# A two-layer decoder trunk on one core: the chunk inverse of the delta rule built ahead as one packed matrix

## The chip, the cores and the metric

The kernel runs on one core of one Trainium2 chip. Everything is float32 at the boundary. The metric is the device time of one execution in microseconds; the time shown of the kernel before is the median of three runs. A core has TensorE (PE, matmuls into PSUM), VectorE (DVE), ScalarE (ACT), GpSimd (POOL) and SyncE (SP); the last two serve here mainly as queues that issue DMAs. Each engine works through its own instructions in the order in which the program lists them.

## The reference

Input is x of 256 tokens by 2048 features. Layer 0 mixes tokens by gated DeltaNet (16 query/key heads, 32 value heads, head size 128), layer 1 by sparse attention; each layer then has a gated MLP with a short convolution (width 5120), two layer norms and a gated embedding. The change lies in layer 0's mixer. Its core is, per value head and chunk of C tokens:

```python
lmat = jnp.where(strict, jnp.einsum('bhncd,bhnsd->bhncs', kb, k) * decay, 0.0)
amat = lmat + jnp.eye(C, dtype=jnp.float32)
rhs = jnp.concatenate([vb, kb * jnp.exp(gc)[..., None]], axis=-1)
sol = lax.linalg.triangular_solve(amat, rhs, left_side=True, lower=True, unit_diagonal=True)
```

`k` is the key after a causal convolution of four taps, silu and division by its norm; `kb` is `beta * k`. What follows from `sol` is a recurrence over the chunks: the values that remain after the state's own prediction (`u` below), the output of each chunk, and the state's update. Every head's output is then normalized, gated by silu(z) and multiplied by `w_o`.

## The kernel before

**Products.** All large matmuls are made exact enough by splitting each float32 operand into a rounded part `hi` and a rest `lo`, both in a rounded format. A weight block (512 KB) is loaded by SP into one of three `raw` buffers, ScalarE makes `hi` (L406), VectorE makes `lo` (L414), and PE multiplies: `wide` columns at L343 and L346 (weights stationary, 256 tokens of both parts streaming), narrow ones at L356 to L359. Small products of the mixer are plain float32 matmuls.

**The order of the work.** Nothing is scheduled by hand. The class `Plan` is a list scheduler that runs when the kernel is built: each piece of work is added with `add(engine, cost, emit, after, take, give, rank, tail)`. `cost` is its assumed time on the engine, `tail` the assumed time until a DMA has landed, `take` and `give` name buffers, and among the pieces that can start the smallest `rank` goes first. The ranks stand in the table `RANK` (L165). The result is a fixed list of instructions for each engine. The large products form one chain in program order (`place`, `multiply`); small PE pieces with rank 1 are put between the weight blocks wherever the plan has them ready.

**The mixer's stages.** The 32 value heads form eight groups of four heads (two key heads each), groups 0 to 3 in batch 0 and 4 to 7 in batch 1. The kernel's chunk is 128 tokens, so there are two halves (`a`), and an inverse of 128 x 128 per head and half.

- `batch(b)` (L826) makes the strict lower matrices `L` for four groups: decays come by DMA from a row table and pass through ScalarE (`decays`, `fade`), the key's squared norms are summed by `squares` (ScalarE squares, PE multiplies by ones, L786), `newton` takes the inverse root, the gram matrix of the keys is a PE product (L863), and for batch 1 ScalarE multiplies `L` by the scales (`dim`) and VectorE by the gram (`weigh`, L880). The 32 x 32 diagonal blocks of `L` are stored to HBM (L890), loaded with one block per partition (L896), inverted there by 31 steps of VectorE (L914, L916) and stored as `tt` (L919).
- `front(g)` (L922) makes what needs the queries: norms, the products of keys and queries, masked and decayed.
- `group(g)` (L961) solves for `u`. It fills the block-diagonal matrix `pm` with the inverses of the 32-row blocks by four DMAs (L991), multiplies `L` by it and masks the result to get `W` (`inverse`, `mask`, L1003), and then solves by rounds: `begin` multiplies the right-hand side by `pm`, ScalarE moves the result to `y0` (L1035), and three times PE multiplies by `W` (`apply`, through `mul` at L959) and VectorE subtracts (`less`, L1050). Since `W` has four blocks by four, three rounds are exact. This is done for half 0; then `cross` takes its part out of half 1's right-hand side and the same is done for half 1.
- After `u`, the output product (L1066, L1067), norms, gating (L1097), transposes on PE (L1106), and the split result in `oT`, which `mixes` multiplies by `w_o`.

The groups are spread over the projections: the loop at L1142 runs, for each group, the columns of values, keys, queries and gates that come next, and `mixes` of the group before, while `group(g)` and `front(g + 1)` are put in between by the plan. PSUM has four banks for the large products, two tagged `sp` and two tagged `bk` for the small ones. `L` has five buffers; one of them is taken as `lt` in batch 0.

**Later stages.** Layer norms are written in `norm` (L1265): VectorE (or ScalarE, by the ranks `even`, `put`, `round`, `held`) evens x, PE transposes it, and the result is split again.

Of the kernel before, what the change touches and what calls it, by code (L numbers as in the profile page):

```python
# [8 lines left out]
F32 = mybir.dt.float32  # L9
# [7 lines left out]
P = 128  # L17
# [146 lines left out]
class Trunk:  # L164
# [16 lines left out]
            'round': 1,  # L181
# [46 lines left out]
    def build(self, out):  # L228
# [5 lines left out]
                                qd=2, qo=2, n21=2, sq=1, L=5, pm=1, W=1, u=1, y0=1, y=2, wq=2,  # L234
# [17 lines left out]
        pm, W = new("pm", [8, P]), new("W", [2, 4, P])  # L252
# [6 lines left out]
        nc.gpsimd.memset(W, 0.0)  # L259
# [565 lines left out]

        def batch(b):  # L826
# [11 lines left out]
            d = [squares(K[g], finished("k", K[g]), lambda ps, i=i: nc.vector.tensor_scalar(  # L838
                ss()[:, 4 * i:4 * i + 4], ps, RMS_EPS, None, op0=ALU.add)) for i, g in enumerate(gs)]
            d, rk = newton(ss, 16, d)  # L840

            def scales():
# [9 lines left out]
                s["tt"] = self.dr.tile([4, 8, 4, 32, 32], F32, tag="tt", name="tt")  # L852
            d = s["d"] = add(V, 1.0, scales, [d, rows["go"]], rank=2)
            stored = []
            for i, g in enumerate(gs):
                box = {}

                def gram(g=g, box=box):
                    ps = box["ps"] = sps("sp", [2, 2, P], "l_ps")
                    for a in range(2):  # L860
                        kt = K[g]()[:, :, a * P:(a + 1) * P]
                        for j in range(2):
                            nc.tensor.matmul(ps[:, a, j], kt[:, j], kt[:, j], start=True, stop=True)  # L863
                p = add(E, 0.9, gram, finished("k", K[g]) + [d], take=["sp"], rank=1)
                grams[g] = p
                for a in range(2):
# [11 lines left out]
                    def weigh(a=a, g=g, box=box):  # L878
                        l = five(L[g]()[:, a])
                        nc.vector.tensor_tensor(l, bcast(box["ps"][:, a], 2, 2), l, op=ALU.mult)  # L880
# [934 lines left out]
```

## Time and profile before

| | before |
|---|---|
| median of three runs | 2794.57 us (2793.72 to 2796.26) |
| the profiled execution | 2794.5 us, span 2792.7 |
| PE busy | 2781.3 us, 15100 matmul records |
| VectorE, ScalarE, POOL busy | 1887.7, 1425.5, 104.9 us |
| granted PE clock | 1.000 |
| moved by DMA | 519.63 MB, mean 186 GB/s |

The span runs from the first to the last instruction of the profiled execution; its time has the start and end of the launch around that. "Busy" is the union of an engine's instructions. Matmuls overlap one another in the records (each lasts until its result is out), so the distance from one start to the next is what PE is occupied for, not the duration shown. Each plain float32 matmul leaves two records. In a row of the timeline the first number is the start in microseconds from the beginning of the span, the second the duration; `x8` means eight records merged.

### The profile page before, as it was taken

The page shows a single profiled execution, that of the slowest core. Times are in us where ns is not written, and L with a number is a line of the kernel's source. Part 1 is how long each engine was busy: PE and PEld are TensorE (multiplying, and loading weights), DVE is VectorE, ACT ScalarE, POOL GpSimd, SP SyncE. Part 2 cuts the span into 40 slices and gives each one's busy share as a digit, 9 for nine tenths or more (in the row PEclk, how much of TensorE's full clock was granted, in tenths as well). Part 3 has the DMA queues.
Part 4 walks back from the last instruction along what each step waited for, and adds up shares of the span by engine and source line. Part 5 has one row for each costly group of instructions (what it writes and reads, how often), then busy time and mean ns, then how long its engine had stood idle before and what let it go on. Part 6 is the DMA issues. An engine that isn't in the chain of part 4 may idle for free.

```text
span 2792.7 us, 39922 instructions
## 1 busy us (share of the span) xinstructions
PE 2781.3 (100%) x15100; PEld 2404.7 (86%) x15100; DVE 1887.7 (68%) x2947; ACT 1425.5 (51%) x2263; POOL 104.9 (4%) x177
## 2 busy tenths in 40 slices
PE   9999999999999999999999999999999999999999
PEld 8888888888888888888888888988888888888887
DVE  7877778776777666666545766776766666654575
ACT  5755665555544555555433444455455555543343
POOL 0100001000000000000000000210000000000000
PEclk9999999999999999999999999999999999999999
DMA  7765656655545766666556557554656666655655
GB/s 223 212 176 166 181 150 185 171 157 167 154 133 167 217 206 209 206 198 189 194 194 221 174 168 226 170 163 158 217 157 193 200 195 192 195 193 191 210 174 189
DMA packets 408929, 519.63 MB, mean 186 GB/s; under 512 B 20348, under 2 KB 298208, under 8 KB 408736
## 3 DMA queue, kind: packets, MB, share of 16 engines
q1 hardware_dynamic: 401424, 499.81, 58.5%
q0 software_dynamic: 6624, 16.68, 2.1%
q8 instruction: 118, 1.93, 0.3%
q14 instruction: 75, 0.61, 0.1%
q10 hardware_dynamic: 688, 0.59, 0.1%
HBM read 512.76 MB, written 7.39 MB: 186 GB/s over the span
## 4 chain that ended last, share of the span: by engine, by line
PE 96%; DVE 2%; DMA 1%; ACT 0%; issue 0%; ACTq 0%; DVEq 0%
PE mm_ps L346 33%; PE mm_ps L343 17%; PE b_ps L359 13%; PE b_ps L356 13%; PE b_ps L357 13%; PE s_ps L959 2%; DMA raw<-in_gdn_w_in 1%; PE o_ps L1067 1%; PE w_ps L959 0%; DVE lo L414 0%; PE ss_ps L786 0%; PE lg_ps L1638 0%; PE sc_ps L1555 0%; PE o_ps L1066 0%; PE l_ps L863 0%; PE v_ps L976 0%
## 5 line engine op out<-in xcount | busy, mean ns | idle before, releaser
L414 DVE TENSOR_TENSOR lo<-raw,hi 128x1024 fp32r<-128x1024 f32 (+1 forms) x906 | 1103.4, 1220 | 683.6 <-ACT hi L406 676.8
L406 ACT ACTIVATE hi<-raw 128x1024 fp32r<-128x1024 f32 (+1 forms) x876 | 922.8, 1054 | 1122.2 <-PE mm_ps L346 519.5
L346 PE MATMUL mm_ps<-xT,hi 128*128 128x512 f32 (+1 forms) x4136 | 1014.0, 393 | 1.6 <-DVE pd L556 1.1
L346 PEld LDWEIGHTS mm_ps<-xT,hi 128*128 128x128 f32 (+1 forms) x4136 | 755.1, 188 | 148.8 <-ACT v L567 1.5
L343 PEld LDWEIGHTS mm_ps<-xT,lo 128*128 128x128 f32 (+1 forms) x4136 | 531.1, 191 | 20.7 <-ACT xb L1310 0.3
L343 PE MATMUL mm_ps<-xT,lo 128*128 128x256 f32 (+1 forms) x4136 | 544.2, 283 | 0.1
L356 PE MATMUL b_ps<-hi,xT 128*128 128x512 f32 (+2 forms) x678 | 260.2, 385 | 0.4 <-ACT hi L406 0.4
L357 PE MATMUL b_ps<-hi,xT 128*128 128x512 f32 (+2 forms) x678 | 257.5, 381 | 0.0
L356 PE MATMUL b_ps<-hi,hTA 128*128 128x512 f32 x512 | 199.2, 389 | 0.0
L357 PE MATMUL b_ps<-hi,hTA 128*128 128x512 f32 x512 | 199.2, 389 | 0.0
L359 PE MATMUL b_ps<-lo,xT 128*128 128x512 f32 (+2 forms) x678 | 180.1, 382 | 0.0
L356 PEld LDWEIGHTS b_ps<-hi,xT 128*128 128x128 f32 x678 | 127.4, 188 | 24.3 <-ACT hi L406 0.8
L357 PEld LDWEIGHTS b_ps<-hi,xT 128*128 128x128 f32 x678 | 127.4, 188 | 23.0
L359 PEld LDWEIGHTS b_ps<-lo,xT 128*128 128x128 f32 x678 | 124.7, 188 | 23.0
L359 PE MATMUL b_ps<-lo,hTA 128*128 128x512 f32 x512 | 136.9, 389 | 0.0
L356 PEld LDWEIGHTS b_ps<-hi,hTA 128*128 128x128 f32 x512 | 96.1, 188 | 20.0
L357 PEld LDWEIGHTS b_ps<-hi,hTA 128*128 128x128 f32 x512 | 96.1, 188 | 20.0
L359 PEld LDWEIGHTS b_ps<-lo,hTA 128*128 128x128 f32 x512 | 96.1, 188 | 19.9
L356 PE MATMUL b_ps<-hi,oT 128*128 128x512 f32 (+1 forms) x258 | 103.5, 401 | 0.0
L357 PE MATMUL b_ps<-hi,oT 128*128 128x512 f32 (+1 forms) x258 | 100.6, 390 | 0.0
L563 DVE SCALAR_TENSOR_TENSOR ac<-pd,cw,ac 128x256 f32<-128x256 f32 x192 | 91.0, 482 | 3.8 <-ACT ac L560 0.2
L1393 DVE SCALAR_TENSOR_TENSOR fac<-fpd,fcw,fac 128x256 f32<-128x256 f32 x160 | 74.2, 482 | 2.6
(320 smaller groups left out, 2458.1 us busy)
## 6 DMA issues: line engine op xcount, KB each, us to landing
raw<-in_gdn_w_in SPq DMA_DIRECT2D x191, 512.0 KB, 4.0
raw<-in_ffn_w_down SPq DMA_DIRECT2D x160, 512.0 KB, 4.1
raw<-in_ffn_w_up SPq DMA_DIRECT2D x158, 512.0 KB, 3.9
raw<-in_ffn_w_gate SPq DMA_DIRECT2D x157, 512.0 KB, 4.4
raw<-in_dsa_w_in SPq DMA_DIRECT2D x72, 512.0 KB, 3.7
raw<-in_gdn_w_o SPq DMA_DIRECT2D x64, 512.0 KB, 3.7
raw<-in_ple_w_gate SPq DMA_DIRECT2D x56, 512.0 KB, 4.4
raw<-in_dsa_w_o SPq DMA_DIRECT2D x32, 512.0 KB, 4.5
```

Source lines behind the costliest of these rows:

```text
L343: nc.tensor.matmul(ps[o][:m, S:], lo[:, k, o * P:o * P + m], xk[:, 0], start=False, stop=e)
L346: nc.tensor.matmul(ps[o][:m], hi[:, k, o * P:o * P + m], xk.rearrange("p a b -> p (a b)"), start=s, stop=e)
L356: nc.tensor.matmul(ps[o][:, c], xh, hi[:, k, c], start=s, stop=False)
L357: nc.tensor.matmul(ps[o][:, c], xl, hi[:, k, c], start=False, stop=False)
L359: nc.tensor.matmul(ps[o][:, c], xh, lo[:, k, c], start=False, stop=e and c.stop == n)
L406: nc.scalar.activation(hi, box["raw"], AF.Copy)
L414: nc.vector.tensor_tensor(lo, box["raw"], box["hi"].bitcast(F32), op=ALU.subtract)
L563: nc.vector.scalar_tensor_tensor(box["ac"], pd[:, k:k + S], wt[:, k:k + 1], box["ac"], op0=ALU.mult, op1=ALU.add)
L959: nc.tensor.matmul(ps[:, h], lhs[:, h], rhs[:, h], start=True, stop=True)
L1067: nc.tensor.matmul(ps[:, h], qd()[:, a, h], u()[:, a, h], start=not a, stop=True)
L1393: x = add(V, 0.48, lambda k=k, pd=pd, ac=ac, m=m: nc.vector.scalar_tensor_tensor(ac(), pd()[:, k:k + S], w["taps"](k, m), ac(), op0=ALU.mu ...
```

## The change

The solve by rounds is replaced by a multiplication with the full inverse, and the full inverse is made ahead, in `batch`, by a new function `solve(s, i)` for each of the four groups. With 32-row blocks, let D be the inverses of the diagonal blocks (known as before) and G the inverse. G's blocks are found from the last block row upwards: for d = 2, 1, 0, the row d of G is minus D of d times the sum over e > d of L[e, d] times row e of G (all transposed, as the kernel holds them). The four heads of a group (and half) are packed: their 32 x 32 blocks stand on the diagonal of one 128 x 128 operand, so that one matmul serves four heads, with 32 to 96 columns streaming.

- `Lb` holds the off-diagonal blocks of `L`, six pairs (e, d) per half. They are stored to HBM by three DMAs per group (`keep`, table `lo`) and fetched by eight (`left`). `L` is free after that; it has four buffers instead of five.
- `Gc` holds G. Its diagonal blocks are fetched from `tt` by eight DMAs, its other blocks come from PE through ScalarE copies.
- `Tb` holds the transposed inverses. They are made by one transposing ScalarE copy per batch, stored as `tu`, and fetched by eight DMAs per group.
- For each d, PE multiplies by `Lb` (`left`), ScalarE copies (`keep`), PE multiplies by `Tb` (`right`), ScalarE negates and copies (`less`). Then one DMA stores Gc.
- `group(g)` fills `pm` with the upper triangle of the inverse by eight DMAs, `begin` multiplies once, and ScalarE copies the result to `u`. `W`, `y0`, `y`, `inverse`, `mask`, `apply` and VectorE's `less` are gone.
- For batch 1 the gram product is issued before the norms, and the squared norms are read from its diagonal by VectorE (`diagonals`), which replaces `squares` for those keys; `weigh` comes before `dim`.
- `front`'s gram product also waits for its decays.
- Fourteen ranks and due times change, and three are new.

The core of the diff:

```diff
-            'due': 3,
-            'tap': 3.6,
-            'rows': 3.5,
+            'due': 2,
+            'tap': 4.5,
+            'rows': 1.5,
-            'solve1': 3.7,
+            'solve1': 5,
-            'weigh1': 3,
-            'dim': 4,
+            'weigh1': 5,
+            'dim': 2,
-            'wild': 5,
+            'wild': 4,
-            'put': 0,
-            'round': 1,
+            'put': 1,
+            'round': 0.6,
-            'held': 0,
-            'even': 8,
-            'last': 0,
+            'held': 1,
+            'even': 16,
+            'last': 1,
-            'free': 2,
-            'after': 4,
-            'cast0': 9}
+            'free': 3,
+            'after': 2,
+            'cast0': 9,
+            'fill': 0.5,
+            'keep': 2,
+            'fetch': 3}
...
+            def diagonal():
+                tmp = new("xt", [256])
+                for n in range(4):
+                    a, j = n // 2, n % 2
+                    nc.vector.scalar_tensor_tensor(tmp[:, :P], box["ps"][:, a, j], 1.0, self.ident, op0=ALU.mult,
+                                                   op1=ALU.mult, accum_out=ss()[:, 4 * i + 2 * j + a:][:, 0:1])
...
+        def solve(s, i):
...
+                def left(q=q, a=a, hs=hs):
+                    nc.gpsimd.dma_start(out=Lb[hs, a, :, hs], in_=s["lo"][i, q])
+                back.append(add(G, 0.55, left, s[i] if not q else [], behind=back[-1:], take=["Lb"] * (not q), tail=3.0, rank=R["keep"]))
...
+            for what in range(2):
+                for q in range(8):
+                    back.append(add(G, 0.55, lambda q=q, what=what: fetch(q, what), [s["u"] if what else s["t"]],
+                                    behind=back[-1:], take=["Tb" if what else "Gc"] * (not q), tail=3.0, rank=R["fetch"]))
+            y = back
+            for d in (2, 1, 0):
+                n = 32 * (3 - d)
...
+                    for a in range(2):
+                        for e in range(d + 1, 4):
+                            nc.tensor.matmul(ps[:, a, 32 * (e - d - 1):], Lb[:, a, PAIR[e, d]], Gc[:, a, e, 32 * e:],
+                                             start=e == d + 1, stop=e == 3)
...
+                    nc.scalar.activation(Gc[:, :, 3, :n], box["ps"], AF.Copy)
...
+                    for a in range(2):
+                        nc.tensor.matmul(ps[:, a], Tb[:, a, d], Gc[:, a, 3, :n], start=True, stop=True)
...
+                    nc.scalar.activation(Gc[:, :, d, 32 * (d + 1):], box["ps"], AF.Identity, scale=-1.0)
+                y = add(E, 0.41 * (3 - d) + 0.05, left, y if d == 2 else [y], take=["bk"], give=["Lb"] * (not d), rank=1)
+                y = add(A, 0.2 + 0.0018 * n, keep, [y], give=["bk"], rank=1)
+                y = add(E, 0.46, right, [y], take=["bk"], give=["Tb"] * (not d), rank=1)
+                y = add(A, 0.2 + 0.0018 * n, less, [y], give=["bk"], rank=1)
...
+            s["st", i] = add(G, 0.6, store, [y], give=["Gc"], tail=3.5)
...
-                L[g] = lazy(lambda: new("L", [2, 4, P], 5))
+                L[g] = lazy(lambda: new("L", [2, 4, P], 4))
...
-            p = add(E, 1.75, gram, qe + finished("k", k) + [d, grams[g]], take=["sp", "sp"], give=["q", "k"], rank=1)
+            p = add(E, 1.75, gram, qe + finished("k", k) + [d, grams[g], *dec], take=["sp", "sp"], give=["q", "k"], rank=1)
...
+            for d in range(4):
+                for a in range(2):
+                    def fill(a=a, d=d):
+                        nc.gpsimd.dma_start(out=pm[32 * d:32 * d + 32, 4 * a:4 * a + 4, 32 * d:],
+                                            in_=s["g", i][:, :, a, d, 32 * d:].rearrange("h j c -> j h c"))
+                    ld.append(add(G, 0.55, fill, [s["st", i]], behind=ld[-1:], take=["pm"] * (not ld), tail=3.0, rank=R["fill"]))
...
-                for n in range(3):
...
-                    def apply(a=a, y=y, box=box):
-                        box["ps"] = sps("bk", [4, P], "s_ps")
-                        mul(W[:, a], y(), box["ps"])
...
-                    def less(nxt=nxt, y0=y0, box=box):
-                        nc.vector.tensor_tensor(nxt(), y0(), box["ps"], op=ALU.subtract)
...
+                d = add(A, 0.6, keep, [x], take=["u"] * (not a), give=["bk"], rank=1)
```

More of the change, by code (lines that the diff above doesn't have):

```diff
@@ L251, in build @@
         w = new("xi", [1024])
-        pm, W = new("pm", [8, P]), new("W", [2, 4, P])
+        pm, Tb, Lb, Gc = new("pm", [8, P]), new("Tb", [2, 3, P]), new("Lb", [2, 6, P]), new("Gc", [2, 4, P])
+        PAIR = {(e, d): e * (e - 1) // 2 + d for e in range(1, 4) for d in range(e)}
         pads = [new(f"pd{i}", [3 + S]) for i in range(2)]
@@ L824, in fade, with gram, product @@
             return r
+        def gram(g, box, deps=()):
+            def product():
+                ps = box["ps"] = sps("sp", [2, 2, P], "l_ps")
+                for a in range(2):
+                    kt = K[g]()[:, :, a * P:(a + 1) * P]
+                    for j in range(2):
+                        nc.tensor.matmul(ps[:, a, j], kt[:, j], kt[:, j], start=True, stop=True)
+            grams[g] = add(E, 0.45, product, finished("k", K[g]) + [*deps], take=["sp"], rank=1)
+            return grams[g]
@@ new lines, in diagonals, with weigh @@
+        def diagonals(g, i, dec, ss):
+            box = {}
+            p = gram(g, box)
+            def diagonal():
[4 more added lines that the diff above has]
+                                                   op1=ALU.mult, accum_out=ss()[:, 4 * i + 2 * j + a:][:, 0:1])
+            d = add(V, 0.9, diagonal, [p], rank=2)
+            for a in range(2):
+                def weigh(a=a):
+                    l = five(L[g]()[:, a])
+                    nc.vector.tensor_tensor(l, bcast(box["ps"][:, a], 2, 2), l, op=ALU.mult)
+                p = dec[a] = add(V, 0.69, weigh, [d, dec[a]], give=["sp"] * a, rank=R["weigh1"])
+            return d
@@ L837, in batch @@
             ss = lazy(lambda: small("kss", 16))
-            d = [squares(K[g], finished("k", K[g]), lambda ps, i=i: nc.vector.tensor_scalar(
-                ss()[:, 4 * i:4 * i + 4], ps, RMS_EPS, None, op0=ALU.add)) for i, g in enumerate(gs)]
+            if b:
+                d = [diagonals(g, i, dec[g], ss) for i, g in enumerate(gs)]
+            else:
+                d = [squares(K[g], finished("k", K[g]), lambda ps, i=i: nc.vector.tensor_scalar(
+                    ss()[:, 4 * i:4 * i + 4], ps, RMS_EPS, None, op0=ALU.add)) for i, g in enumerate(gs)]
             d, rk = newton(ss, 16, d)
@@ L855, in batch @@
             for i, g in enumerate(gs):
[L856 to L865, printed above, removed]
+                box, p = {}, None
+                if not b:
+                    p = gram(g, box, [d])
                 for a in range(2):
@@ L893, in batch, with keep @@
                     stored.append(add(G, 0.6, store, [p], tail=2.5))
+                s[i] = [p]
+                for e in range(1, 4):
+                    def keep(e=e, g=g, i=i):
+                        nc.gpsimd.dma_start(
+                            out=s["lo"][i, :, :, PAIR[e, 0]:PAIR[e, 0] + e].rearrange("q i d j -> i q (d j)"),
+                            in_=L[g]()[32 * e:32 * e + 32, :, :, :32 * e].rearrange("p a h j -> p (a h) j"))
+                    s[i].append(add(G, 0.6, keep, [p], give=["L"] * (e == 3), tail=3.0, rank=R["keep"]))
             ld = lazy(lambda: new("ld", [32, 32]))
@@ L903, in batch @@
             z = add(G, 1.2, clear, [d])
-            lt = lazy(lambda: new("L", [32, 32], 5))
+            lt = lazy(lambda: new("L", [32, 32], 4))
             if not b:
@@ L920, in batch @@
                          [d], tail=4.0)
+            d = add(A, 1.1, lambda: nc.scalar.activation(ld().rearrange("p c j -> p j c"), xi(), AF.Copy), [d], rank=1)
+            s["u"] = add(G, 0.6, lambda: nc.gpsimd.dma_start(out=s["tu"].rearrange("g q b c j -> (g q b) c j"), in_=ld()),
+                         [d], tail=4.0)
+            for i in range(4):
+                solve(s, i)
         def front(g, after=()):
@@ L965, in group @@
             last = g == 7
-            vt = lazy(lambda: new("L" if last else "vt", [2, 4, P], 5 if last else 1))
+            vt = lazy(lambda: new("L" if last else "vt", [2, 4, P], 4 if last else 1))
             key = "k" if last else "v"
```

70 lines of the change are left out of this document (34 added, 36 removed).

## The prediction

> **What bounds the kernel now.** I read the page's totals first, then the chain, then what TensorE (PE) waited for, then the sequence of its instructions.
>
> ```profile
> span 2792.7 us, 39922 instructions
> PE 2781.3 (100%) x15100; PEld 2404.7 (86%) x15100; DVE 1887.7 (68%) x2947; ACT 1425.5 (51%) x2263; POOL 104.9 (4%) x177
> ...
> PE 96%; DVE 2%; DMA 1%; ACT 0%; issue 0%; ACTq 0%; DVEq 0%
> ```
>
> A busy PE is not yet a PE at its peak, so the waits decide. Here are the longest ones of PE and of its weight loads:
>
> ```profile
> PE w_ps L266 <- DVE pd L256: 1.2, 1, 1.2
> PE mm_ps L346 <- DVE pd L556: 1.1, 1, 1.1
> ...
> PEld n_ps L1299 <- DVE x L1287: 2.9, 13, 0.5
> PEld mm_ps L346 <- DVE xT L1328: 1.5, 2, 0.8
> ```
>
> (Each row: who waited for whom, microseconds in all, times, longest.) No wait totals 3 us in 2793. PE is fed from end to end, so the time moves by the PE work that is taken out or put in, plus any wait that is new. VectorE at 68% and ScalarE at 51% of the span bound nothing by themselves.
>
> **The price of the PE work.** The pieces concerned, grouped by operation, and four places in PE's sequence that show what they cost:
>
> ```profile
> L959 PE MATMUL s_ps<-y,W 128*128 128x128 f32 x384 | 50.7, 275 | 0.0
> L786 PE MATMUL ss_ps<-cst,sq 128*128 128x1 f32 x128 | 15.1, 239 | 0.0
> L959 PE MATMUL w_ps<-pm,L 128*128 128x96 f32 x128 | 16.2, 272 | 0.0
> ```
>
> ```profile
> 214.63 1.02 PE L959 MATMUL w_ps<-pm,L 128*128 128x96 f32 x8
> 215.43 1.17 PE L346 MATMUL mm_ps<-xT,hi 128*128 128x512 f32 x4
> 216.44 2.06 PE L343 MATMUL mm_ps<-xT,lo 128*128 128x256 f32 x16
> 218.34 2.00 PE L346 MATMUL mm_ps<-xT,hi 128*128 128x512 f32 x8
> ...
> 227.95 1.98 PE L346 MATMUL mm_ps<-xT,hi 128*128 128x512 f32 x8
> 229.77 0.60 PE L976 MATMUL v_ps<-ident,v 128*128 128x128 f32 x4
> ...
> 574.29 1.05 PE L959 MATMUL s_ps<-y,W 128*128 128x128 f32 x8
> 575.10 1.17 PE L346 MATMUL mm_ps<-xT,hi 128*128 128x512 f32 x4
> 576.11 0.39 PE L356 MATMUL b_ps<-hi,oT 128*128 128x512 f32 x1
> ...
> 609.96 0.95 PE L786 MATMUL ss_ps<-cst,sq 128*128 128x1 f32 x8
> 610.76 2.16 PE L343 MATMUL mm_ps<-xT,lo 128*128 128x256 f32 x16
> 612.76 0.63 PE L346 MATMUL mm_ps<-xT,hi 128*128 128x512 f32 x2
> ```
>
> The durations overlap (matmuls are pipelined), so I price from start to start. Each f32 matmul of the program leaves two records: 8 groups x 2 halves x 3 rounds x 4 heads = 192 products of W, and 384 records. A 512-column record in a run costs (229.77 - 227.95)/8 = 0.2275 us; a 256-column one (218.34 - 216.44)/16 = 0.119. A block of 8 records then costs what it adds until the fourth record after it: 576.11 - 574.29 - 4 x 0.2275 = 0.91 us with 128 columns, 216.44 - 214.63 - 0.91 = 0.90 with 96, and 612.76 - 609.96 - 16 x 0.119 = 0.90 with one column. The width does not matter below 128: 0.113 us a record.
>
> **Removed on PE.** The three rounds of W per half: 384/8 x 0.91 = 43.7 us. The products that make W: 128/8 x 0.90 = 14.4. The sums of squares of keys 4 to 7: four blocks, 3.6. Together 61.7 us. The gram matrices of the keys are only moved ahead of the norms; `begin` keeps its size.
>
> **Added on PE.** `solve` has, per group, 2 x (1 + 2 + 3) products with Lb and 2 x 3 with Tb: 18 matmuls, 36 records; 288 records for 8 groups. Their widths of 32 to 96 columns are not in the trace, but they lie between the 1-column and the 96-column rows, which agree: 288 x 0.113 = 32.5 us. They come as six blocks per group, of 4, 4, 8, 4, 12 and 4 records; should each of the 48 blocks carry 0.1 us of its own, 5 us more. Below, I allow 0.100 us a record, 29 us.
>
> Net on PE: 61.7 - 32.5 = **29.2 us less** (24 to 33).
>
> A rule stands against the flat price: the Trainium skill, "TensorE: Matmul & The Clock Gate", section "Back-to-back issue gap", gives columns/2.4 + 2.5 ns with a floor near 25 ns, an estimated 9 us for all 288 records and some 53 us of gain. The one-column row answers it: 0.90 us for 8 records. Its section on LDWEIGHTS, 128 columns/1.2 = 107 ns whatever streams past, is what the trace agrees with.
>
> **Other engines, all beside PE.**
>
> ```profile
> 0.00:836.00 836.00, 831.63 (x4788) 726.08 (x4789) 627.03 (x1125) 479.67 (x926) 47.15 (x86) 1.00 0.60 173
> ...
> L1050 DVE TENSOR_TENSOR y<-y,s_ps 128x512 f32<-128x512 f32 x32 | 21.9, 685 | 25.0 <-PE s_ps L959 24.9
> ...
> L1035 ACT ACTIVATE y<-s_ps 128x512 f32<-128x512 f32 x16 | 9.5, 596 | 19.2 <-PE s_ps L959 19.2
> ...
> L906 ACT ACTIVATE L<-ld x1: 2073/2073/2073, 119.6 to 119.6; 128x1024 f32<-128x1024 f32 x1
> ```
>
> The first row is the linear-attention stage (engines in the page's order, then clock, DMA share, GB/s). VectorE loses 48 subtractions of 0.685 us (33 us) of 627; the sixteen products that pick the diagonals, even at the price of such a subtraction, bring 11 back. ScalarE gains at most 48 copies of 0.596 us, the price of 512 columns (28.6 us), and two transposing copies of 2.07, on 480 of 836. Both are covered. Bytes added per group: 192 KB kept, 192 for Lb, 224 for Gc and Tb, 512 stored, 320 filled, less 128 filled before; with the second inverse store some 11.5 MB in all, 14 GB/s on 173. Covered by the three raw buffers; uncovered, each weight load that came late would show as a PE wait, of which there is none now.
>
> **The new wait.** A chunk inverse now goes through POOL's queue three times: its 32-row blocks are fetched into Gc and Tb, the packed result is stored, and `pm` is filled from the store. Queued behind a late piece on PE are the weight blocks of the next groups; behind a late piece on POOL, the fetches of the next solve, and for these PE's `begin`.
>
> The DMA view (size, median us to landing), and the landings of the DMAs of `pm`:
>
> ```profile
> pm<-tt POOLq DMA_DIRECT2D x32, 32.0 KB, 3.1
> tt<-xi POOLq DMA_DIRECT2D x2, 512.0 KB, 4.7
> ...
> DMA to landing us min/median/max: 2.0/3.1/6.7
> ```
>
> The timeline of POOL, PE and VectorE around groups 0 and 4 (start, duration):
>
> ```profile
> 159.54 0.56 POOL L919 DMA_DIRECT2D tt<-xi  x1 [44.62 <-DVE ac L563]
> 165.10 2.35 POOL L991 DMA_DIRECT2D pm<-tt  x4 [5.00 <-DMA tt<-xi]
> ...
> 533.52 0.56 POOL L919 DMA_DIRECT2D tt<-xi  x1 [91.46 <-DVE xi L916]
> ...
> 177.15 1.08 PE L959 MATMUL s_ps<-vt,pm 128*128 128x128 f32 x8
> ...
> 202.98 0.69 DVE L1050 TENSOR_TENSOR u<-y,s_ps 128x512 f32<-128x512 f32 x1 [0.57 <-PE s_ps L959]
> ...
> 213.87 1.12 DVE L1097 SCALAR_TENSOR_TENSOR zs<-o_ps,rs,zs 128x128 f32<-128x128 f32 x4
> 225.81 1.38 PE L1106 MATMUL ot_ps<-ident,zs 128*128 128x128 f32 x8 [0.94 <-DVE n L946]
> 240.77 0.48 PE L356 MATMUL b_ps<-hi,oT 128*128 128x512 f32 x1
> ...
> 571.52 1.05 PE L959 MATMUL s_ps<-vt,pm 128*128 128x128 f32 x8
> 577.03 1.05 PE L959 MATMUL s_ps<-y,W 128*128 128x128 f32 x8
> ```
>
> For group 0: the inverse is stored from 159.5 and landed at 165.1. POOL issues in 2.35/4 = 0.59 us each: 16 fetches for Gc and Tb end at 174.5, landed at 177.6 with the median of 3.1. The copy for Tb (2.07 + 0.6 + 4.7 from 159.5: 166.9) is in time. The six products of `solve` alternate with ScalarE copies; one such hop, from a product over its eviction to the next product with weight blocks between, takes 577.03 - 574.29 = 2.74 us: 194.0. Store, 0.6 + 4.7: 199.3. Eight fills, 4.7 + 3.1: 207.1, where `begin` stood at 177.15 before. From there to u took 203.7 - 177.15 = 26.5; six hops fall away (16.4), leaving 10.1: u at 217.2 instead of 203.7, and the output, 213.87 + 1.12 - 203.7 = 11.3 later, at 228.5 instead of 215.0. But the transposes of it ran only at 225.81 then, held for a PSUM bank that `front(1)` had taken (the wait on n L946), and `front` now asks for it after its decays. So they come 2.7 us later, and the first matmul that reads oT, at 240.77, needs them and 4 us of copies: 233. Some 7 us are spare, and PE takes weight blocks meanwhile. Group 4: 533.5 + 47.6 = 581.1 against 571.5, with 16.4 less behind it: not late. The solves of a batch follow one another in 9.4 + 3.1 + 16.4 + 5.3 = 34 us, since Gc is one buffer: group 1's `pm` is full by 199.3 + 34 + 7.8 = 241, about where the 240.77 row stands, again with 16.4 less behind it; later groups gain some 30 us each.
>
> With the slowest landings (6.7 for 3.1 twice, for 4.7 once) the chain grows by 9 us, and 2 us of stall remain per batch; with hops a microsecond longer too, 8. I take 2 us in all, of 0 to 16.
>
> **Ranks and moved steps.** The landings of the weight loads (`raw`) in the first 836 us:
>
> ```profile
> DMA to landing us min/median/max: 3.6/4.0/11.6
> ```
>
> The ranks only order what an engine does next; those of VectorE and ScalarE (`tap`, `due`, `dim`, `weigh1`, `solve1`, `calm`, `wild`, `last`) move work on engines with a quarter or more of their time free. `rows` puts 16 loads of 512 KB two weight blocks earlier on SP's queue, ahead of raw loads; L comes free earlier, after its kept rows land, so SP waits there less. Raw loads in this stage took up to 11.6 us to land with no PE wait on them, so I price it 0, up to 5. The gram of keys 4 to 7 now takes a PSUM bank before its decays are sure to be there and holds it until `weigh`: 0, at worst what `front` cost by the same hold, 1 us each for four. For the norms (`even`, `put`, `round`, `held`), the quoted n_ps and xT waits, 4.4 us, are all that can be won; moving two more pieces to ScalarE at four places could lose as much. 0, within 5.
> **Sum.** The profiled execution took 2794.5 us, 1.8 around its span, and the median is 2794.57. 2794.5 - 29.2 + 2 = **2767**.
>
> **Rivals.** *Narrow matmuls cost by their width.* By rows, 256 columns less save 0.2275 - 0.119 = 0.108 us, so 32, 64 and 96 columns would cost 0.024, 0.038 and 0.051; with 128, 96 and 64 records of them 10 us: 2794.5 - 61.7 + 10 + 2 = 2745. The one-column row speaks against it. 5%. (By the gap rule of the page above, this is what would happen.)
>
> *Half the gain is lost at the batch starts*: the first group of each batch comes 8 us late, and oT, zs and the PSUM pair of the gates with it, so that PE has no free bank to go on in: 2794.5 - 29.2 + 16 = 2781. For it: the old chain was already awaited at 225.81; against: 7 us spare. 13%.
>
> *PE meets the DMAs sixteen times, late*: every group has a first product after the fetches and a `begin` after the fills, placed in PE's written order for a landing of 3.0 us, with all later weight blocks queued behind and VectorE and ScalarE behind those. At the longest landing each is 3.7 us late. From 29.2/16 = 1.8 us each the gain is gone, from 2.2 the kernel is measurably slower; at 2.5 the time is 2794.5 - 29.2 + 40 = 2805. For it: 256 more issues on POOL, in order. Against: eight such meetings exist now, and PE waits for none. 9%. The Trainium skill, "SBUF — State Buffer", section "SBUF: two separate sides", speaks for it: VectorE's two-port copies lock POOL out of writing descriptors; the quoted issues, 0.59 us in every batch of four, show none of it.
>
> *The ranks undo it*, with PE's work gone but the norms slower: within 0.2% of before, 2%.
>
> **Chances.** The forecast has 71%, its own range 2760 to 2776. The range 2752 to 2786 adds the case of the batch starts and the upper price of the records; left out are the cheap records, the slower rival and the tails of the rest, 2 in 10 at most. About 0.2% (5.6 us) is what a measurement of this kernel can tell from no change. Faster: 0.71 + 0.05 + 0.11 = 0.87; same 0.05; slower 0.08.
>
> **What would show it.** PE should have 15100 - 384 - 128 - 32 + 288 = 14844 matmul records; the products with Lb and Tb should cost 0.113 us a record from start to start; PE's waits should stay under some 10 us; the 836 us of the first stage should shrink by about 27 and the rest stay. Wrong would be PE waiting for ScalarE's Gc or for pm (the two late rivals), or n_ps waits grown.

## The result and the profile after

The changed kernel takes 2775.69 us (median of 4 runs, 2770.41 to 2777.85) against 2795.41 for the kernel before beside it: a ratio of 0.9923, with a 95% interval of 0.9911 to 0.9935. It is 19.7 us faster, where 27.5 were forecast. A second series, again beside the kernel before, gave 0.9924 (0.9911 to 0.9936). The profiled execution took 2776.15 us, with a span 18.4 us shorter than before.

The page's totals and chain, as shown of before:

```profile
span 2774.3 us, 39795 instructions
PE 2754.7 (99%) x14844; PEld 2378.9 (86%) x14844; DVE 1855.8 (67%) x2908; ACT 1439.3 (52%) x2314; POOL 250.4 (9%) x437
...
PE 95%; DMA 3%; POOL 1%; DVE 1%; issue 0%; SPq 0%; ACT 0%; ACTq 0%; DVEq 0%
```

The count of matmul records is the forecast 14844. PE is still the bound, but DMAs now take 3% of the chain that ends last, for 1% before, and POOL is new in it. What PE waited for (us in total, times, longest):

```profile
PE b_ps L362 <- ACT hi L412: 3.7, 2, 2.5
PE s_ps L1057 <- DMA pm<-gs: 2.8, 2, 2.2
PE mm_ps L352 <- DVE pd L562: 1.7, 1, 1.7
PE s_ps L894 <- DMA Tb<-tu: 1.4, 1, 1.4
...
PE s_ps L1057 <- DMA Gc<-tt: 0.5, 1, 0.5
```

Weight blocks that come late cost 3.7 us (first row), for 0.4 before. The waits for the operand `pm` and for the fetched blocks Tb and Gc are new, 4.7 us together. (For whom a wait was is inferred from the order of events; the row that names Tb is read again below.)

The price of the new products, from PE's timeline (start, duration):

```profile
637.84 0.53 PE L894 MATMUL s_ps<-Gc,Lb 128*128 128x32 f32 x4
638.21 1.18 PE L365 MATMUL b_ps<-lo,xT 128*128 128x512 f32 x4
...
647.52 1.42 PE L894 MATMUL s_ps<-Gc,Lb 128*128 128x96 f32 x12
648.78 0.48 PE L362 MATMUL b_ps<-hi,xT 128*128 128x512 f32 x1
...
650.69 0.58 PE L903 MATMUL s_ps<-Gc,Tb 128*128 128x96 f32 x4
651.05 0.48 PE L362 MATMUL b_ps<-hi,xT 128*128 128x512 f32 x1
```

From start to start, blocks of 4 and of 12 records take 0.37 and 1.26 us: (1.26 - 0.37)/8 = 0.111 us for each further record. Four records with 32 columns cost 0.37, with 96 columns 0.36: the width does not matter. So the 288 records cost 288 x 0.111 = 32 us and PE's work fell by 61.7 - 32 = 29.7 us. The span fell by 18.4. **Eleven microseconds of new waiting were to be found.**

A view by stretches shows the part that the list of waits does not show. The columns are: stretch, its length, the busy time of PE, its weight loads, VectorE, ScalarE and POOL, then the granted clock, the DMA share and GB/s. Around the wait for `pm` of group 4:

```profile
577.57:580.98 3.41, 3.41 (x17) 2.83 (x16) 2.41 (x4) 3.11 (x6) 2.35 (x5) 1.00 1.03 189
580.98:584.40 3.42, 1.18 (x7) 0.70 (x6) 2.07 (x4) 0.24 (x1) 1.81 (x4) 1.00 1.11 221
584.40:587.81 3.41, 3.41 (x13) 3.02 (x13) 0.43 (x1) 1.71 (x3) 3.36 (x7) 0.50 0.61 173
```

PE is idle for 2.2 us, and then works for 3.41 us at half the clock. That happens three times in this execution, from 185.04, 584.40 and 850.64 us on, and costs about half of 3 x 3.41, 5.1 us, where PE would have been busy. The profiled execution of the kernel before had it only in its last moments.

Where the rest of the gain lies shows at a landmark behind the first stage, the scores of the sparse attention, before and after:

```profile
L1555 PE MATMUL sc_ps<-kiT,qi x64: 270/327/382, 1695.8 to 1776.7; 128*128 128x128 f32 x32, 128*128 128x256 f32 x32
```

```profile
L1624 PE MATMUL sc_ps<-kiT,qi x64: 270/327/382, 1679.2 to 1760.1; 128*128 128x128 f32 x32, 128*128 128x256 f32 x32
```

They start 16.6 us earlier, and 18.4 - 16.6 = 1.8 us more are won behind them. The account: 4.7 for `pm`, Gc and Tb, 3.3 more for weight blocks, 5.1 of half clock, less 1.8: 11.3 us. It is read from one execution of each kernel; how far two executions of the same instructions can differ shows under "The half clock".

### The profile page after: what moved, and what is told of

Read it like the earlier page. It is cut to its first block, busy times and chain, and to the rows that moved or that the text cites. A ratio compares the mean times of both kernels' runs of the same rounds, so it can differ in the third digit from the quotient of the medians.

```text
span 2774.3 us, 39795 instructions
## 1 busy us (share of the span) xinstructions
PE 2754.7 (99%) x14844; PEld 2378.9 (86%) x14844; DVE 1855.8 (67%) x2908; ACT 1439.3 (52%) x2314; POOL 250.4 (9%) x437
## 2 busy tenths in 40 slices
DMA packets 418433, 531.42 MB, mean 192 GB/s; under 512 B 24476, under 2 KB 305792, under 8 KB 418240
## 4 chain that ended last, share of the span: by engine, by line
PE 95%; DMA 3%; POOL 1%; DVE 1%; issue 0%; SPq 0%; ACT 0%; ACTq 0%; DVEq 0%
PE mm_ps L352 33%; PE mm_ps L349 17%; PE b_ps L362 13%; PE b_ps L365 13%; PE b_ps L363 13%; PE s_ps L1057 1%; PE s_ps L894 1%; DMA raw<-in_gdn_w_in 1%; DMA gs<-Gc 1%; PE o_ps L1136 1%; DMA pm<-gs 0%; PE n_ps L1368 0%; PE lg_ps L1707 0%; PE sc_ps L1624 0%; POOL pm L1090 0%; PE s_ps L903 0%
## 5 line engine op out<-in xcount | busy, mean ns | idle before, releaser
L1407 POOL DMA_DIRECT2D lng<-in_ln_g x16 | 8.7, 544 | 1334.0 <-DVE x L1413 1328.1
```

Of the source, the lines that this page charges most:

```text
L1407: d = add(G, 0.55, lambda r=r, src=src: nc.gpsimd.dma_start(out=r(), in_=bass.AP(tensor=src.tensor, offset=src.offset + nb * 512, ap=[[0, ...
```

## The experiments

All times are medians beside the kernel before on the same chip, which took 2795.8 to 2797.2 us; the ratios are to it.

### What the products of the solve cost

`e3`, in both `left` and `right` of `solve`:

```diff
-                    for a in range(2):
-                        nc.tensor.matmul(ps[:, a], Tb[:, a, d], Gc[:, a, 3, :n], start=True, stop=True)
+                    for _ in range(2):
+                        for a in range(2):
+                            nc.tensor.matmul(ps[:, a], Tb[:, a, d], Gc[:, a, 3, :n], start=True, stop=True)
```

> Each matmul block of the chunk solve issued twice into the same bank, so that the solve's 288 records become 576; the planner's costs are unchanged. Theory (a narrow f32 record costs 0.113 us whatever its width, and PE is the bound): PE work +32.5 us, and each solve's chain is 4 us longer, of which up to 4 us at the first and up to 4 us at the fifth group show as longer waits: 2808 to 2817. Rival (narrow records cost by their width, about 0.04 us): +11 us, 2786 to 2790. Rival (the solve hides in waits that PE has anyway): below 2782.

Measured: 2802.78 us, ratio 1.0020 (1.0011 to 1.0029), 27 us above the changed kernel. From its timeline:

```profile
632.66 2.76 PE L895 MATMUL s_ps<-Gc,Lb 128*128 128x96 f32 x24
635.26 0.64 PE L1177 MATMUL ot_ps<-ident,zs 128*128 128x128 f32 x4
```

Twelve more records add 2.60 - 1.26 = 1.34 us, 0.112 each, 32 us for 288. The price by width (11 us) is refuted. The time lies below the 2808 that I expected at least, because the waits did not grow: PE waits for no `pm` in this kernel, and it is idle for 14.6 us of the span against 19.6, which are the 5 us by which the total stays below the added work. My reading is that the longer work brings PE later to DMAs that land as before; no run shows that by itself.

### The ranks

`e1` gives the changed kernel the old values back (the three new names stay); `e2` gives the kernel before the new ones. They are fourteen; the seventeen of the expectations count the three new names with them.

```diff
-  'due': 2, 'tap': 4.5, 'rows': 1.5, 'solve1': 5, 'weigh1': 5, 'dim': 2, 'wild': 4, 'put': 1, 'round': 0.6,
-  'held': 1, 'even': 16, 'last': 1, 'free': 3, 'after': 2
+  'due': 3, 'tap': 3.6, 'rows': 3.5, 'solve1': 3.7, 'weigh1': 3, 'dim': 4, 'wild': 5, 'put': 0, 'round': 1,
+  'held': 0, 'even': 8, 'last': 0, 'free': 2, 'after': 4
```

> The changed kernel with the 17 old rank values (the three new names keep theirs). Theory (PE is the bound; the 17 ranks only reorder work that is hidden): within 3 us of the changed kernel's 2775.7, so 2773 to 2779, with 2730.5 us of PE work as before the edit. Rival 1 (the ranks carry several us of the gain): 2781 or more. Rival 2 (the new ranks cost time, and are where the missing 9 us went): 2771 or less.

> The kernel before with the 17 new rank values and nothing else of the change. Theory (the ranks pay only together with the new chain of products and copies; before has no late chain to help): 2793 to 2799, at most one new wait of 2 to 3 us near 75 us, where the broadcast loads of the decays now go ahead of weight loads. Rival 1 (the ranks are worth their 8 us in any kernel): 2786 to 2789. Rival 2 (the new ranks hurt the old chain, since the order was fitted to the new one): 2800 or more.

Measured: `e1` 2783.73 us, 0.9959 (0.9947 to 0.9972), 8 to 10 us above the changed kernel; `e2` 2795.44, 0.9997 (0.9988 to 1.0005). So the ranks are worth nothing by themselves and some 9 us with the new chain: rival 1 holds for `e1`, the theory for `e2`. PE's waits of `e1`, and a stretch of it:

```profile
PE s_ps L903 <- DMA Tb<-tu: 4.7, 4, 1.6
PE mm_ps L352 <- DVE pd L562: 3.2, 1, 3.2
...
635.82:646.06 10.24, 9.83 (x40) 9.27 (x41) 1.23 (x1) 2.97 (x9) 0.00 (x0) 0.50 0.20 60
```

With the old ranks the products of the solve stand in PE's order before their blocks have landed, four times in two pairs. Behind one pair follow 10.24 us of half clock, as shown, behind the other 3.41. `e2` has one long wait:

```profile
PE b_ps L356 <- ACT hi L406: 3.1, 1, 3.1
```

It stands near 74 us, where the changed kernel waits for a weight block too (1.1 us in its profile, 3.4 in the second one). `rows` puts six broadcast loads of 512 KB in a row on SP ahead of the weight loads. That they cause the wait is not shown: `e1`, with the old ranks, waits 1.7 us there, and `e7` below waits 2.1 us with the instructions of before in their old order, where the profile of before has 0.4.

### The norms from the diagonals

`e5` makes batch 1's norms by `squares` again, and its grams wait for the scales.

```diff
-            if b:
-                d = [diagonals(g, i, dec[g], ss) for i, g in enumerate(gs)]
-            else:
-                d = [squares(K[g], ...) for i, g in enumerate(gs)]
+            d = [squares(K[g], ...) for i, g in enumerate(gs)]
```

> In the changed kernel the norms of keys 4 to 7 are again made from squares on ACT and their sums on PE, and the grams again wait for the scales; the solve and the ranks stay. Theory (the diagonals' worth is the PE work that they save, 3.6 us, since PE is the bound): 2778 to 2781. Rival 1 (also the earlier grams matter, the batch starts later and the fifth group's wait grows): 2782 or more. Rival 2 (the sums hid in waits): 2774 to 2777.

Measured: 2776.09 us, 0.9932 (0.9920 to 0.9944), 2.5 us by the ratios above the changed kernel, with 14876 matmul records, the 32 more. That is near the 3.6 us of PE work, but the intervals do not separate it from nothing: inconclusive.

### Where the waits come from

`e4` only changes the landing times that the planner assumes, `e6` only where four early weight loads of the next stage stand, `e9` adds to `e6` an order on POOL's queue and takes away the planner's allowance (`lag`) between the store and the fills.

```diff
e4:
-  ... take=["pm"] * (not ld), tail=3.0, rank=R["fill"]
+  ... take=["pm"] * (not ld), tail=4.5, rank=R["fill"]      (fetches and loads of Lb alike; store 3.5 to 5.5; tt, tu 4.0 to 5.0)
e6:
-  (9, 10, 11, 12)
+  (10, 11, 12, 13)
e9, in solve, first load of Lb:
-  behind=back[-1:]
+  behind=back[-1:] or ([s["st", i - 1]] if i else [])
e9, in the fills of pm:
+  ... lag=0.0, tail=3.0, rank=R["fill"]
```

> Only the planner's landing times change: fetches and fills 3.0 to 4.5 us, the store of the solved blocks 3.5 to 5.5, the two transposed stores 4.0 to 5.0, so that PE's products are placed later among the projections. Theory (the missing gain is two waits of 1.4 and 2.2 us for DMAs that land later than planned, each followed by some 3.4 us at half clock): both waits and both stretches of half clock go, 4 to 7 us less than the changed kernel, 2769 to 2772. Rival (PE has nothing else ready there, the wait only moves): 2774 to 2778, with a wait of 1.5 us or more still behind a fetch or a fill.

> One edit in the changed kernel: the four early weight loads of the next stage are placed one block later, so that one more load of the output projection goes ahead of them on SP's queue. Theory (PE's wait of 2.5 us at 848 us is for a projection load that stood behind an early load whose buffer was not free, and the half clock after it is a consequence): the wait falls under 1 us and the half clock there goes, 3 to 4 us less than the changed kernel, 2771.5 to 2773. Rival (the wait only moves by one block): 2775 to 2777.

> The edit of the early weight loads, and a second one: the loads of the next group's solve factors wait on POOL's queue until the store of this group's solved blocks is issued, so the store goes out about 4.5 us earlier (the planner then also puts the fills of the operand ahead of the next fetch). Theory (the fifth group's wait of 2.2 us for its operand is eight issues of 0.55 us that stood ahead of the store): that wait and its half clock go too, about 4 us less than with the first edit alone, 2766 to 2769. Rival 1 (the wait is for the landings themselves, 4 to 5.5 us each, or only moves): 2770.5 to 2773. Rival 2 (the later loads make the next solve late): 2774 or more.

`e4`: 2776.24 us, 0.9926 (0.9913 to 0.9940), no gain. Its waits between 60 and 400 us (there is none between 560 and 640):

```profile
PE s_ps L894 <- DVE zs L1166: 2.7, 1, 2.7
PE b_ps L362 <- ACT hi L412: 2.4, 1, 2.4
PE mm_ps L352 <- DVE pd L562: 1.7, 1, 1.7
PE b_ps L362 <- DVE hi L416: 1.7, 1, 1.7
```

Both waits that it aimed at are gone. Others of the same size stand in batch 0, three of them with half clock behind them: one near 74 us, which the changed kernel has too, and two that it has not, for `hi` at 187 us and for `zs` at 242 us, in the planner's new order. So the assumed landings were too short, and the total does not show it.

`e6`: 2771.54 us, 0.9911 (0.9897 to 0.9924), 4 us below the changed kernel's median, with overlapping intervals. PE has no wait from 836 to 870 us in it. But in the changed kernel's second profile the wait near 850 us was only 0.6 us without any edit, and `e5` and `e12`, which leave these loads alone, have none over 0.2 us there. It comes and goes, and that `e6` removes it is not shown.

`e9`: 2774.93 us, 0.9924 (0.9910 to 0.9937), no better than `e6`, perhaps worse. POOL's timeline shows why:

```profile
571.34 0.57 POOL L914 DMA_DIRECT2D gs<-Gc  x1 [17.57 <-ACT Gc L906]
571.90 3.94 POOL L869 DMA_DIRECT2D Lb<-lo  x7
...
579.03 1.09 POOL L1090 DMA_DIRECT2D pm<-gs  x2 [0.75 <-DMA Lb<-lo]
581.85 1.09 POOL L1090 DMA_DIRECT2D pm<-gs  x2 [1.73 <-DMA Lb<-lo]
```

The loads of Lb now stand between the store and the fills, and the fills stop for 0.75 and 1.73 us until such loads have landed. My theory, that eight issues ahead of the store made the wait, is refuted. The changed kernel's own rows show why: its last copy into Gc ends at 567.25 us and the store goes out at 568.53, so the eight loads of Lb hold it back by 1.3 us and not by 4.5.

`e10` takes `e6` and the longer landings for batch 1 alone; `e11` adds to it that the first fronts' broadcast loads go behind more weight loads.

```diff
e10:
-  ... tail=3.0, rank=R["fill"]
+  ... tail=4.5 if b else 3.0, rank=R["fill"]
e11, in decays:
+  behind=[order[19 + g * 2]["load"], *ahead] if back and g < 2 else ahead if back else ()
```

> The edit of the early weight loads, and the longer landings in the planner for the second batch of four groups alone (4.5 us for fetches and fills, 5.5 for the store, 5.0 for the transposed stores), so that the first batch keeps its order. Theory (the fifth group's wait of 2 us is a landing that the planner put too short; the same edit in the first batch only bought other waits): the wait near 582 us falls under 0.5 us and its half clock goes, 3 to 4 us less than with the early loads' edit alone, 2767 to 2769. Rival (the planner's other order makes other waits there): 2770.5 or more.

> As the kernel with the second batch's landings, and on SP's queue the broadcast load of the first front's decays (0.5 MB) goes behind one more weight load, that of the second front behind three. Theory (PE's wait near 75 us is for a weight load that stood behind six broadcast loads in a row): that wait falls from 2 to 3 us to under 1.2 us and its half clock goes, 2 to 4 us less, 2763 to 2767. Rival (the four loads for the batch's decays do it alone, or the second front is late now): 2768 or more.

> The changed kernel once more, beside the next three on one chip. Theory: 2771 to 2779; waits and stretches of half clock near 75, 171 to 185, 582 and 848 us, and none of either over 1 us between 860 us and the end.

`e10`: 2769.40 us (2766.90 to 2770.32), 0.9901 (0.9887 to 0.9914). The changed kernel on the same chip took 2775.83 (2771.62 to 2777.70): 6.4 us more, and the two sets of times do not meet. `e10` beats both kernels. How the 6.4 us divide between its two edits is not shown: its ratio lies 0.0010, 2.8 us, below that of `e6`, and these intervals overlap. Its stretch around group 4, to be read against the three rows above:

```profile
560.00:630.00 70.00, 70.00 (x413) 61.70 (x412) 44.50 (x75) 38.92 (x79) 27.50 (x51) 1.00 0.66 186
```

PE is never idle in it and the clock stays at 1.00. The wait near 184 us is still there (1.6 us, with 3.41 us of half clock). Its profiled span of 2765.1 us is 27.6 below that of before.

`e11`: 2770.78 us, 0.9907 (0.9893 to 0.9921), no gain over `e10`. The wait near 74 us is still there (2.0 us, for a `hi` from VectorE), and the one for `pd` at 174 grew to 2.6. What sets the wait near 74 us stays open.

### The half clock

`e7` takes the kernel before, whose profile has none until its end, and makes 18 pauses on PE with a chain of POOL instructions that leaves the weights as they are:

```diff
+                if kind == "hi" and ks[0] == 2 and "gap" in b:
+                    one = box["hi"][:, 1:3, 0:8]
+                    nc.gpsimd.tensor_copy(one, one)
+                    for _ in range(b["gap"]):
+                        nc.gpsimd.memset(self.pause, 0.0)
+                    nc.gpsimd.tensor_copy(one, one)
                 b["emit"](box["hi"], box.get("lo"), kind, ks, last)
```

> The kernel before, whose clock is 1.0 throughout, with 18 made pauses on PE in the two feed-forward stages, 44 us apart: a POOL copy of a few weights onto themselves stands between two matmul pieces, with 0, 1, 2, 3, 4, 6, 8, 11 and 14 small memsets behind it (the second stage in the opposite order). Pauses from about 0.8 to 3 us are expected, about 30 us in all. Theory (the granted clock is set for each 3.41 us stretch of a fixed grid by how idle PE was in the stretch before; the traces so far have no half clock up to 1.24 us idle, both outcomes at 1.4 to 1.7, always half from 1.8): a stretch of 3.41 us at half clock follows every pause that leaves over 1.8 us idle in one stretch and none that leaves under 1.3, and each costs 1.7 us beside the pause. Rival 1 (only pauses of a whole stretch, 3.4 us, do it, and the drops so far have another cause, such as the load of the DMAs): none of the 18 does it. Rival 2 (the length of the pause alone decides, whatever the grid): one sharp length for all 18.

Measured: 2832.72 us, 1.0135 (1.0121 to 1.0149), 36.9 us more. The profiled execution was the slowest of four, 2839.77 us, with a span 45.3 us longer than before. In it the made pauses took 28.1 us (first row):

```profile
PE mm_ps L350 <- POOL hi L427: 28.1, 18, 3.3
...
PE b_ps L360 <- ACT hi L410: 2.1, 1, 2.1
```

Four of them, all over 2.6 us, brought half clock, one for two stretches: 5 x 1.7 = 8.5, together 36.6 of the 45.3. Of the other 8.7 us, 5.3 come before the first pause. Up to there PE, VectorE and ScalarE run the instructions of before in the same order, and yet PE waits 2.1 us near 74 us (second row, 0.4 in the profile of before) with half clock behind it, and the last product of the first stage starts at 886.3 instead of 881.0. So two executions of one order can differ by 5 us in this stage; a wait that one profile has and another has not is not yet the work of an edit. The last 3.4 us stay open.

Two of the other made pauses, 2.01 us each, did not. Two stretches of each kind:

```profile
1221.21:1224.63 3.42, 1.70 (x11) 1.17 (x9) 2.58 (x6) 0.75 (x2) 1.49 (x9) 1.00 0.60 169
1224.63:1228.04 3.41, 3.12 (x14) 2.58 (x15) 0.64 (x1) 1.06 (x1) 1.82 (x5) 1.00 0.89 220
...
1269.01:1272.42 3.41, 0.78 (x4) 0.29 (x2) 1.80 (x3) 0.45 (x2) 2.23 (x13) 1.00 0.77 230
1272.42:1275.83 3.41, 3.27 (x8) 2.59 (x9) 0.00 (x0) 1.02 (x1) 0.57 (x2) 0.50 0.76 177
```

1.72 us idle in a stretch: no. 2.63: half clock in the next. The length of a pause alone does not decide: in the changed kernel's second profile a wait of 2.78 us for `pm`, as long as the pause of the last two rows (2.77), fell across the edge of two stretches:

```profile
584.29:587.70 3.41, 2.03 (x9) 1.34 (x8) 2.32 (x5) 1.86 (x3) 1.63 (x3) 1.00 1.12 213
587.70:591.11 3.41, 2.01 (x13) 1.86 (x14) 0.93 (x3) 0.84 (x2) 2.80 (x6) 1.00 0.86 241
591.11:594.52 3.41, 3.41 (x21) 2.93 (x20) 3.41 (x8) 1.53 (x3) 3.16 (x6) 1.00 0.20 34
```

1.4 us idle in each, and no half clock. On the other hand, a wait for `pm` of only 1.85 us in `e6` lies within one stretch, 582.23 to 585.64, and half clock follows. The theory holds; both rivals fall.

`e12` fills that wait with work that is overwritten:

```diff
+                    for n in range(16 if g == 4 and not a else 0):
+                        nc.tensor.matmul(box["ps"][:, n % 4], self.ident, self.ident, start=True, stop=True)
                     mul(pm[:, 4 * a:4 * a + 4], vt()[:, a], box["ps"])
```

> The changed kernel with 16 small products of the unit matrix (1.8 us of PE work that is overwritten) put into the fifth group's wait for its operand, between 581 and 584 us. Theory (PE's idle share of the stretch before sets the clock): the wait left idle is under 0.7 us, no half clock follows near 584 us, and the whole is 0 to 2 us faster although PE does more. Rival (the half clock comes from something else there, such as the DMAs or the f32 products): it stays, and the time is the same or up to 1.8 us more.

Measured: 2775.27 us, 0.9921 (0.9908 to 0.9935). Each product leaves two records, so the filling took 3.57 us, not 1.8:

```profile
588.76 3.73 PE L1119 MATMUL s_ps<-ident 128*128 128x128 f32 x32
592.33 0.83 PE L1057 MATMUL s_ps<-vt,pm 128*128 128x128 f32 x6
```

PE does not wait for `pm` any more, no half clock follows, and 3.6 us of useless work cost no time that can be measured. Since the second profile shows the same place without half clock too, this supports the theory but does not decide; `e7` does.

## Why the prediction was right, and where it was not

The time of 2775.69 us lies in the stated range, near the upper end of the forecast's own. That it lies there is owed to the width of the ranges: the work was priced to half a microsecond, but 11.3 us were lost to waits and half clock where the sum had 2. One sign of being wrong did appear, PE waiting for `pm`; no product waited long for ScalarE's Gc, and the n_ps waits did not grow.

**What bounds the kernel, and the price of the work: right.** PE was and is the bound; the records are those forecast; a narrow record costs 0.111 against 0.113 us, the net 29.7 against 29.2. The rival by which narrow records cost by their width is refuted by the blocks and by `e3`. The sentence from the Trainium skill on which it leaned ("TensorE: Matmul & The Clock Gate", "Back-to-back issue gap", a floor near 25 ns) does not describe these products. The same page's section "LDWEIGHTS (loading the stationary operand)" has columns/1.2, an estimated 107 ns for 128 columns of weights, which is near the 0.111 us of the rows. But the weight loads' own records last 0.19 us here, so why a narrow record costs 0.111 us is not shown.

**The other engines and the bytes: right.** VectorE and ScalarE bound nothing. 531.42 MB moved against 519.63 before, 11.8 more for 11.5 forecast.

**The new wait: mis-sized, 2 us against 4.7, and 6.1 in the second profile.** Two steps of it failed. The first is "Group 4: 533.5 + 47.6 = 581.1 against 571.5, with 16.4 less behind it: not late." The operand came at 584.2. POOL's queue, and PE where it waits:

```profile
568.53 0.58 POOL L914 DMA_DIRECT2D gs<-Gc  x1 [0.42 <-issue]
574.23 0.56 POOL L878 DMA_DIRECT2D Gc<-tt  x1 [5.11 <-DMA gs<-Gc]
574.77 3.79 POOL L1090 DMA_DIRECT2D pm<-gs  x7
579.58 0.55 POOL L1090 DMA_DIRECT2D pm<-gs  x1 [1.01 <-DMA Gc<-tt]
```

```profile
581.57 0.39 PE L363 MATMUL b_ps<-hi,oT 128*128 128x512 f32 x1
584.20 1.86 PE L1057 MATMUL s_ps<-vt,pm 128*128 128x128 f32 x8 [2.24 <-DMA pm<-gs]
```

The store took 5.1 us to land where I had 4.7; a fetch for the next group goes ahead of the fills; the eighth fill stops until that fetch, eight issues earlier, has landed; and it lands 4.6 us after its issue for my 3.1. Another 1.3 us is a later start, as the inverse was stored at 534.85 for 533.52. PE was there at 582.0, so a landing at 581.1 would have done, but my reason for "not late" was no reason: the 16.4 us behind `begin` are spare for those who wait for `u`, while PE itself stands at `begin` in its written order. Lateness had to be taken against PE's own arrival.

The second is "16 fetches for Gc and Tb end at 174.5, landed at 177.6 with the median of 3.1." POOL again, PE in the first solve, and the landing of the one fetch at 176.11:

```profile
176.11 0.55 POOL L878 DMA_DIRECT2D Gc<-tt  x1 [1.62 <-DMA tu<-ld]
176.90 3.79 POOL L875 DMA_DIRECT2D Tb<-tu  x7 [0.24 <-DMA Gc<-tt]
184.72 0.55 POOL L875 DMA_DIRECT2D Tb<-tu  x1 [4.02 <-DMA Tb<-tu]
```

```profile
184.57 0.38 PE L894 MATMUL s_ps<-Gc,Lb 128*128 128x32 f32 x2 [1.44 <-DMA Tb<-tu]
```

```profile
DMA to landing us min/median/max: 8.3/8.3/8.3
```

The row of PE names Tb, but PE goes on at 184.57, before the last fetch of Tb is even issued (184.72). The product reads Gc, and the eighth fetch of Gc, issued at 176.11, lands 8.3 us later, at 184.43. That is what PE waited for. In all five profiles in which PE waits at this product (both of the changed kernel, `e3`, `e10`, `e11`) it goes on 0.13 or 0.14 us after this landing. POOL's stop of 4.02 us ends with the same landing, since that fetch lies eight issues earlier.

Three things made it late. The inverse went out 5.0 us later (164.56 for 159.54). The fetch stopped for 1.62 us until the copy for Tb, eight issues earlier, had landed. And its landing took 8.3 us for my 3.1. That 3.1 was the median over all fills of before; the four fills at this very place took longer there already:

```profile
DMA to landing us min/median/max: 5.5/6.0/6.7
```

In the changed kernel the DMA engines are fuller there as well. The same stretch, before and then after (the last two columns are the DMA share and GB/s):

```profile
170.00:184.00 14.00, 14.00 (x99) 12.89 (x99) 9.32 (x17) 7.99 (x21) 0.00 (x0) 1.00 0.62 181
170.00:184.00 14.00, 11.44 (x72) 9.91 (x71) 8.50 (x15) 9.38 (x24) 8.17 (x15) 1.00 1.04 313
```

SP issues four loads of `L` for batch 1 in a row from 167.94 us on, 512 KB each, where before issued one at a time. That this crowding makes the landing so long is argued and not shown.

`e4` and `e10` show that the wait at group 4 is a matter of the landings that the planner assumes: with 4.5 us it is gone in both, and PE comes to `begin` 3 us after the last fill has landed. In `e4` the wait of the first product is gone too.

**Weight loads, "0, up to 5": 3.7 and 4.0 us in the two profiles, 0.4 before.** I had named the step (`rows` ahead of raw loads) and let the long landings of before, which PE did not feel, stand for those to come. How much of it the change makes is open: `e2` has the wait near 74 us with the ranks alone, but `e7` has it without them (2.1 us), and the one near 850 us comes and goes.

**Ranks, "0, within 5": right on the kernel before (`e2`), wrong on the new one, 8 to 10 us (`e1`).** The step that failed is that ranks only move work on engines with time to spare. They decide when a piece of a chain is ready, and so whether PE stands before it. In the same words the rival that the ranks undo the gain is refuted. Of the 27 us forecast for the first stage 15.1 came: its last product with `oT`, behind the 836 us that the forecast named, starts at 881.0 before and at 865.9 after. The 3.3 won behind it, where the norms are, lie inside the bound.

**The half clock: not in the sum at all.** 5.1 us in both profiles of the changed kernel. A stall of 2.2 us cost 3.9, with the 1.7 of half clock behind it.

**The rivals of the late batches** were mechanisms that did happen, at a smaller size: one batch start of two by 2.2 us, and of the sixteen meetings two over 1 us late, three in the second profile. The forecast of 2767 is near what the changed kernel gives when the wait of group 4 is planned away and the early loads stand one block later: `e10`, 2769.4. Part of that nearness is luck, since `e10` still waits at the first solve and has half clock behind it.

## What to carry to other kernels

When a change takes work off the engine that bounds a kernel, that engine arrives earlier at everything that hangs on a DMA: take each landing against the new arrival, and give a planner the landings of the trace (here 4 to 5.5 us for 3.0 and 3.5). Read them at the place concerned and not as a median over the kernel: at the first solve the fills took 6 us before, for a median of 3.1, and one fetch 8.3 after. That longer landings should be planned only where they bind is what `e4` and `e10` suggest, but the two differ in the early loads too. Price a stall on PE with the half clock that may follow. And when a chain is new, tune the order and the chain together: the same ranks were worth nothing in the old kernel and some 9 us in the new one.

## What the runs showed of the hardware

The granted clock goes by a fixed grid of 3.413 us. The drops of the first profile, at 185.04, 584.40 and 850.64 us, lie 117 and 78 times that apart, and all others of one execution fit such a grid. Over the profiles of before, the changed kernel (twice) and eleven experiments I took, for each stretch of the grid at full clock, how long PE was idle in it. Between 20 and 2700 us, among stretches without products of the solve, 49 with 0.70 to 1.73 us idle were followed by full clock, all of them; 21 with 1.76 us or more by half clock, all of them. At the two ends of a program two stretches fall outside: half clock after 1.57 us at the start of `e11`, none after 1.80 us at the end of `e2`. In stretches with the narrow products of the solve the bound can lie lower: half clock after 1.04, 1.44, 1.60, 1.63 and 1.67 us, none after 1.28 and 1.44. Why is open. It lasts one stretch, sometimes two or three, even where PE is hardly idle (10.24 us in `e1`, with PE busy for 9.83 of them).

The Trainium skill, "TensorE: Matmul & The Clock Gate", section "Part 1: The HAM clock gate", has a free-running window of 3413 ns, and the traces agree. By its words the clock falls after at least one idle window, and its section on HAM oscillation warns of gaps above some 3.4 us; here about half a window was enough, and the measurement decides.

On POOL's queue an issue waits until the DMA eight issues before it has landed, as the stops of 1.01, 1.62 and 4.02 us above show; in none of the fourteen profiles does an issue start before that landing. A series of sixteen small DMAs can therefore go no faster than eight in the time of one landing.
